# Summing four products of a weight pair in one PSUM bank, with ScalarE copies between, in a two-level feed-forward and mixer kernel

## The chip, the cores and the metric

The kernel runs on one core of a Trainium2 chip. The metric is the device time of one launch in microseconds (us), the median of several runs. Five engines work beside each other: TensorE (PE in the profile) multiplies into PSUM banks, VectorE (DVE), ScalarE (ACT) and GpSimd (POOL) work on tiles, and SyncE (SP) issues most of the DMAs.

## The reference, cut to what matters

One layer of a diffusion backbone over 1024 latent tokens and 256 context tokens, width 1024, in fp32. The three projections that the change touches are the inputs of the two feed-forward nets (1024 to 2 x 2816, then `silu(a) * b`) and the convolution and gate part of the mixers' input (1024 to 5 x 1024).

```python
def swiglu(h, w_in, w_out):
    a, b = jnp.split(h @ w_in, 2, axis=-1)
    return (jax.nn.silu(a) * b) @ w_out

def conv_branch(bg, cg, vc, conv_w):
    return bg * short_conv(cg * vc, conv_w)

x = x + 0.5 * ml[2] * swiglu(modulate(rms_norm(x, norm1_g), ml[0], ml[1]), ffn1_w_in, ffn1_w_out)
bg_l, cg_l, vc_l, q_l, k_l, v_l, gt_l = jnp.split(hx @ w_in, SPLITS, axis=-1)
g_conv, g_attn = jnp.split(jax.nn.sigmoid(gate_logits), 2, axis=-1)
x = x + ml[5] * merged
x = x + 0.5 * ml[8] * swiglu(modulate(rms_norm(x, norm3_g), ml[6], ml[7]), ffn2_w_in, ffn2_w_out)
```

## The kernel before, in words

Every fp32 product is made of three fp32r passes (high x high, high x low, low x high), so that one 128 x 512 output of 512 inputs takes 4 x 3 = 12 matmuls; `product` (line 683) issues them into one PSUM bank of its own. Each weight is split into a high part (a cast on ScalarE, tile `wl`) and a low part (a subtraction on VectorE, the same tile's second half); `wl` has four buffers, `raw` (the weights as loaded) three.

The class `Winograd` (line 487) computes the three projections with the seven-product scheme of Strassen and Winograd on 2 x 2 blocks: two halves of the tokens (C0 and C1) times two halves of the inputs, for a pair of 128-column weight blocks. The moving operands 0 to 7 (tiles `r`) are made once per stage in `norm0` and `norm1`; the weight sums `s1`, `s2`, `s3` are made per pair on GpSimd in `lefts` (line 613). There are three users: `half1` (first feed-forward, 22 pairs), `mix` (20 pairs) and `fast` (second feed-forward, 22 pairs). The first 13, 9 and 9 pairs of these have products 1 and 2 made **ahead**, while the norm of C1 is still being made (`start_by_half`, `start`), and their sums `u` (product 1) and `c` (products 1 + 2) kept: the first two on the chip, the others in DRAM (`ucd`), from where `fetch` (line 750) brings them back a pair early. An ahead pair thus has five products left, another pair seven.

For each pair the loop runs `next_first`, `second`, `third` (lines 758 to 776). They put the products in the order 6, 7, 4, 5, 3 (1 and 2 first where not ahead), each in one of five `ps` banks, and combine them on VectorE: u += 6, v = u + 7, b = v - 4, then v += 5, u += 5, u += 3. The results for C0 are c and b, those for C1 u and v. `spill` (line 1164) takes silu of one and multiplies, and stores the product; in `mix`, `mixed` and `gate` do the corresponding thing. From pair 14 (`SIDE_FROM`) on, `half1` also has `side` work: each weight that goes by serves the context tokens too, in a `po` bank, and product 0's weight is called for in between.

A scheduler fixes the order of every engine's instructions at build time; it follows the program order with freedom where data allow. On the chip each engine then works through its list in that order, waiting at each instruction for what it needs. Small generators (`steps`, `mix_steps`, `last_steps`) put the work of later stages, such as the modulation sums `macc` and the final loads, between the pairs.

Of the kernel before, what the change touches and what calls it, by code (L numbers as in the profile page):

```python
# [12 lines left out]
AF = mybir.ActivationFunctionType  # L13
# [27 lines left out]
SIDE_FROM = 14  # L41
# [10 lines left out]
def tile_dit_layer(  # L52
# [434 lines left out]
    class Winograd:  # L487
# [6 lines left out]
        def __init__(self, xs, gain, mod, m, pairs, plain=False, ahead=3, side_from=None):  # L494

            self.xs, self.gain, self.mod, self.m, self.plain = xs, gain, mod, m, plain
            self.halves, self.cols_a = [], [a for a, _ in pairs]
            self.r = {i: [None] * 4 for i in range(8)}
            self.side_from = side_from
            self.n_ahead, self.side, self.started, self.n_left = ahead, None, [], 0
            self.n_squares, self.accs = {}, {}
            self.source, self.ready = self.lefts(pairs, side_from), []

# [43 lines left out]
        def norm1(self, turned=None):  # L552
# [60 lines left out]
        def lefts(self, pairs, side_from):  # L613

            def cols(src):
                t = wpool.tile([P, SLOT], F32, tag="raw", name=uniq("raw"), bufs=3)
                load(t[:].rearrange("p (k n) -> p k n", n=P), src.rearrange("(k p) n -> p k n", p=P))
                return t[:, :512], t[:, 512:]
# [24 lines left out]
            for j, (wa, wb) in enumerate(pairs):  # L643
                side = side_from is not None and j >= side_from
                a, b = cols(wa), cols(wb)
# [4 lines left out]
                if j >= n:  # L650
                    yield from map(parts, a)
                yield parts(s2)
                yield parts(s3)
                if side:
                    yield parts(b[0])
                yield parts(b[1])
                yield parts(s1)
                pool.tensor_sub(out=s2, in0=a[1], in1=s2)
                yield parts(s2)
                if side_from is not None and j == side_from - 1:  # L660
                    for wa, wb in pairs[:side_from]:
                        yield from map(parts, cols(wa) + cols(wb))

        def prefetch(self, n, lo_engines=(None, None)):
            while len(self.ready) < n:
# [7 lines left out]
            self.prefetch(4)  # L673
            return self.ready.pop(0)

        def terms(self, ps, w, i, k):
            r = self.r[i][k]
            wh, wl = (w[:, v, k * P : (k + 1) * P] for v in range(2))
            matmul(ps, wh, r[:, 0], start=k == 0, stop=False)
            matmul(ps, wh, r[:, 1], start=False, stop=False)  # L680
            matmul(ps, wl, r[:, 0], start=False, stop=k == 3)

        def product(self, i):
            w, ps = self.left(), ps_s()
            for k in range(4):
                self.terms(ps, w, i, k)
            if self.side:
                self.side(i, w)
            return ps

        def first(self):

            u, c = ttile("u"), ttile("c")
            act.copy(out=u, in_=self.product(1))
            dve.tensor_add(out=c, in0=u, in1=self.product(2))
            return u, c

        def start(self, norm):

# [55 lines left out]
                    load(t, self.started[0][:, i])  # L755
                self.started[0] = u, c

        def next_first(self):
            if not self.started:
                return self.first()  # L760
            self.fetch()
            uc = self.started.pop(0)
            self.fetch()
            return uc

        def second(self, u):

            v, b = ttile("v"), ttile("b")
            dve.tensor_add(out=u, in0=u, in1=self.product(6))
            dve.tensor_add(out=v, in0=u, in1=self.product(7))  # L770
            if self.side:
# [12 lines left out]
    class Rows:  # L784

# [354 lines left out]
    def side(j, bank=ps_o):  # L1140
# [20 lines left out]

        return do

    def spill(a, b, j, ch):
# [9 lines left out]
    def context_out(j, banks=None, first=True, last=True):  # L1174
# [18 lines left out]
        for half in range(2):  # L1193
            for token in range(2):
# [3 lines left out]
                acc = c_acc[token][:, half * 512 : (half + 1) * 512]  # L1198
                dve.tensor_add(out=acc, in0=acc, in1=ps)

    for j in range(NH):
        half1.side = side(j) if j >= SIDE_FROM else None
        u, c = half1.next_first()
        v, b = half1.second(u)
        spill(c, b, j, C0)
        spill(*half1.third(u, v), j, C1)
# [94 lines left out]
        sp.dma_start(out=xc.t[i][:].rearrange("p a b -> p (a b)"), in_=cxd[i])  # L1301
    normc2 = modulated_norm(xc, h_ctx[0], h_ctx[1], CC, gain2, mods, 3)

    def mixed():
        u, a0 = mix.next_first()
        v, b0 = mix.second(u)
        a1, b1 = mix.third(u, v)
        return (C0, a0, b0), (C1, a1, b1)
# [462 lines left out]
    ]  # L1771

    fast.start(fast.norm1())
    for j in range(NH):
        if j > 1:
            run(last_steps, 3)
        u, c = fast.next_first()
        v, b = fast.second(u)
        spill(c, b, j, C0)
        spill(*fast.third(u, v), j, C1)  # L1780
    run(last_steps)
    gate3 = half_gate("gate3", 8)
    hs = Rows(hd, NH // 2, "hid")
# [76 lines left out]
```

## Time and profile before

| what | value |
|---|---|
| median of three runs | 2682.8 us (2680.39 to 2686.76) |
| the profiled execution's own time, and its span | 2685.79 us, 2684.0 us |
| mean granted TensorE clock | 0.995 |
| busy: PE, DVE, ACT, POOL | 98%, 75%, 44%, 21% |
| pairs: `half1` ahead / with side work | about 122 to 300 us / 457 to 677 us |
| pairs: `mix` | about 951 to 1250 us |
| pairs: `fast` | about 2072 to 2450 us |

A row of groups gives an engine, an operation, its tiles, how often (x), the sum in us and the mean in ns of one, then the idle time of the engine just before and what ended it. A row of windows gives the busy time of PE, PE's weight load, DVE, ACT and POOL in a stretch, then the clock, the share of DMA and GB/s. A row of the chain gives a start, a length, and the engine and tile that the end of the program was waiting for then.

### The profile page before, as it was taken

The numbers are of one execution on the slowest core, as the hardware profiler recorded it, in microseconds if no ns is written. First come the engines' busy times: TensorE is split into PE (matmuls) and PEld (weight loads), VectorE is DVE, ScalarE is ACT, GpSimd is POOL, SyncE is SP. The second block draws the span as 40 slices with busy tenths as digits, with TensorE's granted clock in tenths as the row PEclk, the third lists the DMA queues.
The fourth block names the chain that finished last, engine by engine and source line by source line (L and its number), as shares of the span: only waits on it lengthen the run. The fifth ranks groups of instructions, "written<-read, shape, count | busy, mean of one in ns | idle before, by whom it ended". The sixth has DMA issues, their size and how long they took to land.

```text
span 2684.0 us, 36956 instructions
## 1 busy us (share of the span) xinstructions
PE 2639.7 (98%) x13373; PEld 2221.6 (83%) x13373; DVE 2006.2 (75%) x3356; ACT 1171.3 (44%) x2317; POOL 557.9 (21%) x449
## 2 busy tenths in 40 slices
PE   8999999999999999999999999999999999999998
PEld 5787899888778878888999888887888788888888
DVE  5788966888877899877387676675668876667885
ACT  6533454433444633333245566673236233334453
POOL 0134201211010044333032112141001442330200
PEclk9999999999999999999999999999999999999999
DMA  8565465345974345242312532113734543228741
GB/s 317 194 204 177 144 221 173 109 130 209 288 182 122 111 158 180 95 130 75 103 48 91 87 87 64 32 44 110 262 100 144 181 154 95 86 88 288 182 90 64
DMA packets 370000, 376.93 MB, mean 140 GB/s; under 512 B 19590, under 2 KB 258328, under 8 KB 369816
## 3 DMA queue, kind: packets, MB, share of 16 engines
q1 hardware_dynamic: 359000, 353.03, 40.8%
q0 software_dynamic: 10816, 21.53, 4.9%
q8 instruction: 105, 1.72, 0.3%
q14 instruction: 79, 0.65, 0.1%
HBM read 306.78 MB, written 67.67 MB: 140 GB/s over the span
## 4 chain that ended last, share of the span: by engine, by line
PE 84%; DVE 4%; DMA 2%; issue 2%; POOL 1%; ACT 1%; SPq 0%; DVEq 0%; POOLq 0%; ACTq 0%
PE ps L90 69%; PE pt L90 7%; PE po L90 7%; DVE wl L90 1%; DMA raw<-in_ffn_w_in_dram 1%; DMA ws<-in_ffn_w_out_dram 1%; DVE r L90 1%; DMA rawm<-in_w_mod_dram 1%; POOL s L90 0%; DVE macc L90 0%; POOL ol L90 0%; DVE u L90 0%; DVE uc L90 0%; DVE nt L90 0%; DVE v L90 0%
## 5 line engine op out<-in xcount | busy, mean ns | idle before, releaser
L90 PE MATMUL ps<-r,wl 128*128 128x512 f32 x5196 | 1204.7, 391 | 12.2 <-DVE wl L90 5.3
L90 PEld LDWEIGHTS ps<-r,wl 128*128 128x128 f32 x5196 | 971.6, 188 | 221.9 <-DVE wl L90 7.9
L90 ACT CAST wl<-s 128x512 fp32r<-128x512 f32 x254 | 156.7, 619 | 322.6 <-PE ps L90 219.3
L90 POOL TENSOR_TENSOR s<-raw 128x512 f32<-128x512 f32 x64 | 93.4, 1459 | 891.2 <-DMA raw<-in_ffn_w_in_dram 380.9
L90 ACT CAST wl<-raw 128x512 fp32r<-128x512 f32 x287 | 177.5, 619 | 219.6 <-PE ps L90 157.3
L90 DVE TENSOR_TENSOR wl<-raw,wl 128x512 fp32r<-128x512 f32 x287 | 201.9, 705 | 62.1 <-ACT wl L90 59.6
L90 DVE TENSOR_TENSOR wl<-s,wl 128x512 fp32r<-128x512 f32 x254 | 229.8, 905 | 21.3 <-ACT wl L90 19.7
L90 POOL TENSOR_TENSOR s<-raw,s 128x512 f32<-128x512 f32 x64 | 103.9, 1624 | 362.3 <-DVE wl L90 362.3
L90 DVE SCALAR_TENSOR_TENSOR macc<-rawm,silu_c,macc 128x512 f32<-128x512 f32 x178 | 149.8, 858 | 31.7 <-DMA rawm<-in_w_mod_dram 30.7
L90 PE MATMUL ps<-wh,r 128*128 128x256 f32 x768 | 141.6, 285 | 0.0
L90 DVE TENSOR_TENSOR u<-u,ps 128x512 f32<-128x512 f32 x174 | 118.0, 678 | 28.7 <-PE ps L90 28.5
L90 DVE TENSOR_TENSOR pts<-pt,pts 128x512 fp32r<-128x512 f32 x160 | 108.7, 685 | 35.7 <-ACT pts L90 33.5
L90 ACT CAST pts<-pt 128x512 fp32r<-128x512 f32 x160 | 93.3, 595 | 94.8 <-PE pt L90 90.9
L90 DVE TENSOR_REDUCE m<-ps 128x1 f32<-128x512 f32 (+1 forms) x192 | 109.9, 594 | 23.3 <-PE ps L90 22.3
L90 ACT CAST rh<-hid 128x512 fp32r<-128x512 f32 x132 | 80.9, 620 | 101.6 <-PE ps L90 89.3
L90 PE MATMUL ps<-rh,wl 128*128 128x512 f32 x360 | 122.3, 390 | 2.8 <-ACT rh L90 2.8
L90 PEld LDWEIGHTS ps<-wh,r 128*128 128x128 f32 x768 | 120.6, 192 | 0.0
L90 PE MATMUL po<-pts,vh 128*128 128x512 f32 x256 | 111.4, 440 | 0.2 <-ACT pts L90 0.2
L90 PE MATMUL ps<-wl,r 128*128 128x256 f32 x384 | 108.8, 283 | 0.0
L90 ACT CAST wh<-raw 128x512 fp32r<-128x512 f32 (+1 forms) x85 | 67.9, 801 | 88.8 <-PE ps L90 57.8
L90 DVE TENSOR_TENSOR rl<-hid,rh 128x512 fp32r<-128x512 f32 x132 | 89.8, 684 | 20.2 <-PE ps L90 9.8
L90 PE MATMUL ps<-kl,qs 128*128 128x512 f32 x384 | 104.3, 395 | 0.0
(314 smaller groups left out, 5118.6 us busy)
## 6 DMA issues: line engine op xcount, KB each, us to landing
raw<-in_ffn_w_in_dram SPq DMA_DIRECT2D x130, 512.0 KB
raw<-in_ffn_w_out_dram SPq DMA_DIRECT2D x72, 512.0 KB
rawm<-in_w_mod_dram SPq DMA_DIRECT2D x136, 256.0 KB
raw<-in_w_in_dram SPq DMA_DIRECT2D x61, 512.0 KB
hid<-hd SPq DMA_DIRECT2D x40, 512.0 KB
ws<-in_ffn_w_out_dram POOLq DMA_DIRECT2D x30, 512.0 KB, 6.6
ucd<-uc SPq DMA_DIRECT2D x25, 512.0 KB
hd<-c SPq DMA_DIRECT2D x40, 256.0 KB
```

The source lines that it names most:

```text
L90: inst = getattr(self.engine, name)(*args, **kw)
```

## The change

Product 4's moving operand changes its sign (operand 4 is now f minus t2), so that product 4 can be added by TensorE. A pair now has two banks, x and z:

- x is opened by product 1, or for an ahead pair by a ScalarE copy of the kept `u` into the bank. Product 6 is added onto it; ScalarE copies the sum out (`u6`). Product 7 is added on; ScalarE copies the sum out (`v`). Product 4 is added on, and x is now b, which the multiply (or the sigmoid, into a tile of its own) reads from PSUM.
- z takes product 5, then v += z on VectorE; product 3 is added onto z, then u6 += z on VectorE.

The order of products is 5, 7, (side 0), then the head of the next pair (its 6 where ahead, its 1 and 2 elsewhere), 4, 3, then the next pair's 6 where that has not come yet. `order` in `lefts` writes this order for the weights, `results` for the products. Between pair 13 and pair 14 of `half1` the pairs stay apart. The three loops take results from the generator `results` instead of calling `next_first`, `second` and `third`.

```diff
@@ class Winograd
-                dve.tensor_sub(out=t2, in0=t2, in1=f[:, 1])
+                dve.tensor_sub(out=t2, in0=f[:, 1], in1=t2)
                 self.keep(4, k, t2)
...
-    def second(self, u):
-        v, b = ttile("v"), ttile("b")
-        dve.tensor_add(out=u, in0=u, in1=self.product(6))
-        dve.tensor_add(out=v, in0=u, in1=self.product(7))
-        if self.side:
-            self.side(0, self.left())
-        dve.tensor_sub(out=b, in0=v, in1=self.product(4))
-        return v, b
-    def third(self, u, v):
-        p5 = self.product(5)
-        dve.tensor_add(out=v, in0=v, in1=p5)
-        dve.tensor_add(out=u, in0=u, in1=p5)
-        dve.tensor_add(out=u, in0=u, in1=self.product(3))
-        return u, v
+    def head(self, j):
+        if j >= self.n_pairs:
+            return None
+        if j < self.n_ahead:
+            self.fetch()
+            u, c = self.started.pop(0)
+            x = ps_s()
+            act.copy(out=x, in_=u)
+            self.fetch()
+            return x, self.with_sixth(x), c
+        u, c = ttile("u"), ttile("c")
+        x = self.product(1, j=j)
+        act.copy(out=u, in_=x)
+        dve.tensor_add(out=c, in0=u, in1=self.product(2, j=j))
+        return x, None, c
...
+    def with_sixth(self, x):
+        u = ttile("u6")
+        act.copy(out=u, in_=self.product(6, x))
+        return u
+    def results(self, apart=None):
+        opened = self.tail(self.head(0))
+        for j in range(self.n_pairs):
+            x, u, c = opened
+            z, v = self.product(5), ttile("v")
+            act.copy(out=v, in_=self.product(7, x))
+            dve.tensor_add(out=v, in0=v, in1=z)
+            side = self.sides(j)
+            if side:
+                side(0, self.left())
+            if j + 1 != apart:
+                opened = self.head(j + 1)
+            self.product(4, x, j)
+            yield c, x
+            self.product(3, z)
+            dve.tensor_add(out=u, in0=u, in1=z)
+            if j + 1 != apart:
+                opened = self.tail(opened)
+            yield u, v
+            if j + 1 == apart:
+                opened = self.tail(self.head(j + 1))
...
-    def gate(dst, j, ch, g):
-        act.activation(out=g, in_=g, func=AF.Sigmoid)
+    def gate(dst, j, ch, src):
+        g = ttile("gate")
+        act.activation(out=g, in_=src, func=AF.Sigmoid)
```

The first place is ScalarE's list in the middle of `fast`'s ahead pairs. Before, one pair has its five weight casts (`wl_20094`, `wl_20114`, `wl_20132`, `wl_20164`, `wl_20182` for products 6, 7, 4, 5, 3) and the two silu, and no copy:

```order
L90 CAST wl_20094<-s_3717_20089 128x512
L90 CAST wl_20114<-s_3718_20090 128x512
L90 CAST wl_20132<-raw_20086 128x512
L90 CAST wl_20164<-s_3716_20088 128x512
L90 ACTIVATE c_20159<-c_20159 128x512
L90 ACTIVATE u_19925<-u_19925 128x512
L90 CAST wl_20182<-s_3717_20089 128x512
```

Now it reads as follows (`u_3561_19701` from its bank is a `u6`, `ps_19810` from `u` is the copy that opens the next x, `v_19677` is the copy after a product 7, `wl_19678` is the weight of a product 3, `wl_19702` and `wl_19718` those of the next pair's 5 and 7, `wl_19746` that of the 6 after):

```order
L90 CAST wl_19678<-s_3535_19534 128x512
L90 COPY v_19677<-ps_19590 128x512
L90 CAST wl_19702<-s_3550_19635 128x512
L90 COPY u_3561_19701<-ps_19695 128x512
L90 CAST wl_19718<-s_3552_19637 128x512
L90 COPY ps_19810<-u_19697 128x512
L90 ACTIVATE c_19698<-c_19698 128x512
L90 CAST wl_19746<-s_3567_19741 128x512
```

Three copies have come into each ahead pair's list, each behind at most one cast; the copy that opens a bank and the silu of the reloaded `c` stand ahead of the cast for that pair's product 6.

The second place is PE's list where `fast` begins. Before, products 6, 7, 4, 5 of the first pair run through each other in four banks (`ps_19706` is 6, `ps_19724` is 7, `ps_19751` is 4, `ps_19771` is 5), as the last quarter of each operand comes in:

```order
L90 MATMUL ps_19724<-r_3580_19416,wl_19665 128x512 x3
L90 MATMUL ps_19724<-r_3597_19483,wl_19665 128x512 x3
L90 MATMUL ps_19771<-r_3564_19352,wl_19703 128x512 x2
L90 MATMUL ps_19751<-r_3566_19359,wl_19682 128x512
L90 MATMUL ps_19751<-r_3583_19426,wl_19682 128x512 x3
L90 MATMUL ps_19751<-r_3600_19493,wl_19682 128x512 x3
L90 MATMUL ps_19724<-r_3612_19544,wl_19665 128x512
L90 MATMUL ps_19771<-r_3564_19352,wl_19703 128x512
L90 MATMUL ps_19771<-r_3581_19419,wl_19703 128x512 x3
```

Now (`ps_19526` is x, with `wl_19469` for 6 and `wl_19507` for 7; `ps_19559` is z, with `wl_19490` for 5):

```order
L90 MATMUL ps_19559<-r_3467_19243,wl_19490 128x512 x3
L90 MATMUL ps_19559<-r_3484_19310,wl_19490 128x512 x3
L90 MATMUL ps_19559<-r_3499_19371,wl_19490 128x512
L90 MATMUL ps_19526<-r_3500_19374,wl_19469 128x512
L90 MATMUL ps_19559<-r_3499_19371,wl_19490 128x512 x2
L90 MATMUL ps_19526<-r_3500_19374,wl_19469 128x512 x2
L90 MATMUL ps_19526<-r_3449_19173,wl_19507 128x512 x3
L90 MATMUL ps_19526<-r_3466_19240,wl_19507 128x512 x3
```

Only two products run through each other; 7 follows on the bank of 6 with nothing between them.

The third place is PE's list at the end of `fast`, products 7 (`wl_22174`) and 4 (`wl_22191`) of the last pair, which has no next pair behind it:

```order
L90 MATMUL ps_22124<-r_3483_19307,wl_22174 128x512 x3
L90 MATMUL ps_22124<-r_3498_19368,wl_22174 128x512 x3
L90 MATMUL ps_22124<-r_3452_19183,wl_22191 128x512 x3
L90 MATMUL ps_22124<-r_3469_19250,wl_22191 128x512 x3
L90 MATMUL ps_22124<-r_3486_19317,wl_22191 128x512 x3
```

Before, each product there had a bank of its own; now the copy of `v` has to come between the second and the third of these rows.

More of the change, by code (lines that the diff above doesn't have):

```diff
@@ L504, in __init__ @@
             self.side_from = side_from
-            self.n_ahead, self.side, self.started, self.n_left = ahead, None, [], 0
+            self.n_ahead, self.sides, self.started, self.n_left = ahead, lambda j: None, [], 0
+            self.n_pairs = len(pairs)
             self.n_squares, self.accs = {}, {}
@@ L642, in lefts, with fetch @@
                 yield from map(parts, cols(a))
-            for j, (wa, wb) in enumerate(pairs):
-                side = side_from is not None and j >= side_from
-                a, b = cols(wa), cols(wb)
+            state = {}
+            def fetch(j):
+                if j >= len(pairs) or j in state:
+                    return
+                a, b = map(cols, pairs[j])
                 s1, s2, s3 = ttile("s1"), ttile("s2"), ttile("s3")
@@ L1162, in side, with side_at @@
         return do
+    side_of = {}
+    def side_at(j):
+        if j is None or j < SIDE_FROM:
+            return None
+        if j not in side_of:
+            side_of[j] = side(j)
+        return side_of[j]
+    half1.sides = side_at
     def spill(a, b, j, ch):
@@ L1199, in context_out @@
                 dve.tensor_add(out=acc, in0=acc, in1=ps)
+    results = half1.results(SIDE_FROM)
     for j in range(NH):
[L1202 to L1206, printed above, removed]
+        for ch in (C0, C1):
+            spill(*next(results), j, ch)
         run(steps, STEPS[min(j, len(STEPS) - 1)])
@@ L1773, in tile_dit_layer @@
     fast.start(fast.norm1())
+    results = fast.results()
     for j in range(NH):
@@ L1776, in tile_dit_layer @@
             run(last_steps, 3)
[L1777 to L1780, printed above, removed]
+        for ch in (C0, C1):
+            spill(*next(results), j, ch)
     run(last_steps)
```

87 lines of the change are left out of this document (51 added, 36 removed).

## The prediction

> **What bounds the kernel now.** I read the page's busy times and its chain of waits first: which engine is the program waiting for?
>
> ```profile
> PE 2639.7 (98%) x13373; PEld 2221.6 (83%) x13373; DVE 2006.2 (75%) x3356; ACT 1171.3 (44%) x2317; POOL 557.9 (21%) x449
> PE 84%; DVE 4%; DMA 2%; issue 2%; POOL 1%; ACT 1%; SPq 0%; DVEq 0%; POOLq 0%; ACTq 0%
> 2295.00 182.27 PE ps L90 x804
> ```
>
> TensorE is busy for 98% of the span and owns 84% of the chain. The third row is an uninterrupted piece of the chain in the second feed-forward: 182.27 / 804 = 0.2267 us for one 128x512 matmul. So a product (12 matmuls) costs 2.72 us, an ahead pair (five products) 13.6 us, another pair (seven) 19.0 us. The change issues exactly the same matmuls: it can move the time only by the time in which TensorE waits. What waits does it have, and where? The waits of PE, then the windows of the stages that the change touches:
>
> ```profile
> PE ps L90 <- DVE wl L90: 5.3, 5, 2.8
> PE ps L90 <- ACT r L90: 3.5, 4, 1.6
> PE ps L90 <- ACT wl L90: 2.5, 4, 1.0
> ...
> 122.00:300.00 178.00, 172.93 (x751) 139.20 (x750) 143.53 (x203) 55.79 (x98) 68.80 (x46) 0.99 0.57 179
> 457.00:677.00 220.00, 220.00 (x1152) 187.24 (x1151) 175.08 (x269) 83.65 (x143) 39.45 (x27) 1.00 0.46 154
> 951.00:964.00 13.00, 9.54 (x38) 6.61 (x37) 12.84 (x18) 5.41 (x10) 5.52 (x3) 1.00 0.44 143
> 964.00:1250.00 286.00, 285.57 (x1261) 235.49 (x1261) 241.18 (x354) 92.79 (x163) 105.49 (x70) 1.00 0.41 130
> 2072.00:2093.00 21.00, 18.06 (x75) 13.59 (x75) 20.11 (x25) 8.69 (x16) 7.75 (x5) 1.00 0.33 112
> 2093.00:2447.00 354.00, 354.00 (x1563) 292.60 (x1563) 244.89 (x338) 116.34 (x193) 115.76 (x80) 1.00 0.42 131
> 2447.00:2475.00 28.00, 28.00 (x125) 23.21 (x124) 21.18 (x30) 12.46 (x22) 0.90 (x1) 1.00 0.98 361
> ```
>
> The windows are, in order: the first feed-forward's ahead pairs, its pairs with side work, the start of the mixers' projections, the rest of these, the start of the second feed-forward, the rest of it, and its end. In the three long ones TensorE stands still for 0, 0.43 and 0 us: nothing can be gained there. There are three places with idle time. Ahead pairs: 178.00 - 751 x 0.2267 = **7.75 us** (5.07 by the busy time alone). Start of the mixers: 13.00 - 9.54 = **3.46 us**, with VectorE busy 12.84 of 13.00. Start of the second feed-forward: 21.00 - 18.06 = **2.94 us**, VectorE 20.11 of 21.00. The whole sum is 14.2 us, 0.5% of the span, and that is the most that any relief of VectorE in these places can bring.
>
> **What the change removes and adds.** The groups of the combining instructions and of ScalarE's copies out of a bank:
>
> ```profile
> L90 DVE TENSOR_TENSOR u<-u,ps 128x512 f32<-128x512 f32 x174 | 118.0, 678 | 28.7 <-PE ps L90 28.5
> L90 DVE TENSOR_TENSOR v<-u,ps 128x512 f32<-128x512 f32 x58 | 39.5, 680 | 23.6 <-PE ps L90 23.5
> L90 DVE TENSOR_TENSOR b<-v,ps 128x512 f32<-128x512 f32 x64 | 43.8, 685 | 45.7 <-PE ps L90 44.4
> L90 ACT COPY u<-ps 128x512 f32<-128x512 f32 x33 | 19.4, 587 | 43.0 <-PE ps L90 36.3 <-DMA hd<-u 5.3 <-DVE u L90 1.3
> L90 ACT CAST wl<-s 128x512 fp32r<-128x512 f32 x254 | 156.7, 619 | 322.6 <-PE ps L90 219.3
> ```
>
> Each of the 64 pairs had six additions on VectorE after its products 6, 7, 4, 5 (two) and 3; now it has two. That is 64 x 4 x 0.68 = 174 us less for VectorE (2006 to 1832). ScalarE gets three copies in each of the 31 ahead pairs (u into x, u6, v) and two in the 33 others (u6, v; they copied product 1 before too): 159 x 0.59 = 94 us more (1171 to 1265). No row of before has ScalarE writing a bank; the nearest are its copy out of one, 0.587, and its cast between SBUF tiles, 0.619, and I take 0.59. None of it is on the path by itself, since both engines have room. What counts is the new order on bank x: 7 must wait for the copy after 6, and 4 for the copy after 7. Three cases:
>
> *Steady pairs: 0.* Between 6 and 7 TensorE has the previous pair's 4 and 3 and this pair's 5 (8.2 us); between 7 and 4 it has the next pair's 6 (2.72 us) or its 1 and 2 (5.4 us); between 5 and 3 at least three products. The copy of v stands behind at most one cast in ScalarE's list, so it ends about 0.62 + 0.59 = 1.21 us after product 7, and 2.72 covers it with 1.5 us to spare, the time of two more casts. Queued behind this copy are the casts for products three and four places on (8 us), so 0.59 does not reach TensorE. Without the cover, the price is 0.59 to 1.21 us a pair. The pairs with side work have 220.00 of 220.00 now and can only lose: between nothing and 0.59 in each of 8 pairs, 4.7 us; the cover is longer there, so I take 0.
>
> *Three places without cover.* The end of the second feed-forward: 4 follows 7 directly, because there is no next pair. ScalarE's list has three casts of the next weights ahead of that copy, which may be done by then: 0.59 at the least, 3 x 0.62 + 0.59 = 2.4 at the most, **+0.9** taken, nearest to the copy alone. The starts of the mixers and of the second feed-forward need the chain's rows:
>
> ```profile
> 954.03 0.63 ACT r L90
> 954.68 2.64 DVE r L90 x3
> ...
> 2077.09 5.21 DVE r L90 x5
> 2082.33 1.66 DVE nt L90
> 2084.01 0.63 ACT r L90
> 2084.66 0.69 DVE r L90
> ```
>
> Here TensorE waits for VectorE to make the last operands. Before, four products of the first pair were begun side by side, and three quarters of each, 36 matmuls, were there to do meanwhile. Now there are only 6 and 5 (18 matmuls): 7 comes after 6 is whole and copied. At 2085.4 us, when the last operand is ready, before has nearly all 48 matmuls behind it; after would have 24 and part of 7. If the operands for 6 and 5, which stand first in VectorE's order, let 7 begin near 2083, TensorE is one product (2.72 us) behind, and gets back the 0.9 us that the rest of this window loses now (7.00 - 6.14 between 2086 and 2093): **+1.8**. Bounds: -2.94 (all idle time goes, as VectorE has fewer additions) to 24 x 0.2267 = +5.4.
>
> ```profile
> 2086.00:2093.00 7.00, 6.14 (x27) 4.78 (x26) 6.83 (x10) 2.59 (x5) 1.30 (x1) 1.00 0.10 37
> ```
>
> At the mixers' start the operands come within 5 us (954 to 958.9), so less work can be put off: **+0.4**, one exposed copy less a part of VectorE's relief; bounds -3.46 to +2.72, one product.
>
> The Trainium skill, "PSUM — Partial Sum Buffer", section "PSUM bank collisions raise a hardware error", says that no two engines may touch a bank in the same partitions at once, so that the copy can't run beside the next product's matmuls into the same bank. By that rule the three exposed copies cost their full length; if a copy could overlap the next product's first matmuls, the sum would be lower by up to 3 x 0.59 = 1.8 us. No run here shows such an overlap.
>
> *Ahead pairs of the first feed-forward.* This is where a gain can come from. VectorE is busy 143.53 of 178.00 us and loses 13 x 4 x 0.68 = 35 us of work. But what does TensorE wait for there? Four successive pieces of the chain of this window:
>
> ```profile
> 256.38 5.42 DMA raw<-in_ffn_w_in_dram
> 261.83 1.27 POOL s L90
> 263.19 2.86 POOL s L90 x2
> 266.07 0.63 ACT wl L90
> ```
>
> It is a weight load, then GpSimd's sums, then a cast; VectorE enters only because it holds the raw buffers until the low part is made, and through `macc`. So its relief lets loads start sooner, but does not shorten them. I take half of the 7.75: **-3.9**. Bounds: -7.75, and on the other side each of the 11 reloaded pairs' casts later by one copy, 11 x 0.59 = +6.5.
>
> **Sum.** -3.9 (ahead pairs) + 0.4 (mixers' start) + 1.8 (second feed-forward's start) + 0.9 (its end) = -0.8 us. From the profiled execution's 2685.8 that is 2685.0. That execution lay 3.0 us above the median of the runs (2682.8), so the forecast is **2682 us**. The likeliest case's own range is 2674 to 2691, not all bounds being reached at once.
>
> **Rivals.**
>
> *VectorE's relief counts fully (faster).* All of the 7.75 goes, and the mixers' start and the second feed-forward's lose half their idle time instead of gaining waits (-1.7 and -1.5), the end +0.9: -10, **2673 us**. For it: VectorE is over 95% busy in both starts. Against: in the largest place the chain shows loads and GpSimd. Chance 0.22.
>
> *The copy that opens x blocks ScalarE (slower).* That copy needs the reloaded `u`, and stands ahead of the casts for that pair's 6 and 4. Before, only silu of the reloaded `c` could block so:
>
> ```profile
> ACT c L90 <- DMA c<-ucd: 53.6, 13, 8.5
> ```
>
> Thirteen waits of 4.1 us on average, and TensorE is hardly touched by them, as weights are split two to three products in advance. Now `u` must be there before 6 instead of after it. The case decides where the reload lands so late that the cast for 6 is not done when TensorE comes: that is from 2.72 us (one product of cover) on. With 13 such waits, 13 x (4.1 - 2.72) = +18 us, **2700 us**; with half of them 2691. For it: the first feed-forward moves 179 GB/s and its loads take over 5 us. Against: `c`'s waits occur in the same places now, without loss. Chance 0.20.
>
> *The starts lose a whole product or two.* Upper bounds at both starts, +2.7 and +5.4, with the gain of -3.9 gone: +9.0, **2692 us**. Chance 0.13.
>
> *The change does nothing.* The waits of the ahead pairs are the loads' alone and stay as they are, the starts come out even, the end +0.9: **2684 us**. Chance 0.12.
>
> *The clock falls.* The row of the ahead pairs shows 0.99, the others 1.00, even across the wait of 2.8 us. If new short waits at the bank changes let the granted clock go to half for the time of one pair, it costs 13.6 us: **2696 us**. Chance 0.03. The Trainium skill, "TensorE: Matmul & The Clock Gate", section "A second HAM failure mode: psum-queue depth-cycling", describes that: small idle times between groups of matmuls that cycle through PSUM banks make the clock swing between half and full. The trace speaks against it so far, with 1.00 over 354 us of such cycling.
>
> **How the numbers follow.** The forecast's case has 0.30. The lower end of the range takes in the fast rival with a margin of 2 us: 2671. The upper end is between the slow rival's half and whole price: 2698. Outside lie about 0.06 below and 0.11 above. About 0.2%, 5.4 us, is what a measurement of this kernel can tell from no change: below 2677.4 lie most of the fast rival and a little of the forecast's case, 0.24; above 2688.2 the two slow rivals, the clock and a little of the forecast's, 0.33; between them 0.43.
>
> **What would show it.** VectorE near 1832 and ScalarE near 1265 us busy. PE full (at most 0.5 us idle) in the windows of the steady pairs; a wait of PE for ScalarE's `v` in these would refute the cover. PE waits named `u` or `v` at the two starts and once at the end, under 1.3 us each. In the ahead pairs of the first feed-forward idle time about half of now, with loads and GpSimd still in the chain; if it vanishes, VectorE was the cause. New waits of ScalarE at the bank for the reload of `u`, followed by PE waiting for `wl`, would be the slow rival.

## The result and the profile after

The changed kernel takes 2722.6 us (median of four runs, 2719.1 to 2723.5), the kernel before 2682.8: a ratio of 1.0145, 95% interval 1.0127 to 1.0162. It is **40 us slower**; the forecast was no change, and its range ended at 2698. The profiled execution took 2722.1 us with a span of 2720.3, 36.3 us more than that of before. The page's busy times:

```profile
PE 2652.5 (98%) x13373; PEld 2228.0 (82%) x13373; DVE 1847.0 (68%) x3100; ACT 1250.0 (46%) x2476; POOL 541.4 (20%) x449
```

VectorE and ScalarE do as much as was worked out (1832 and 1265 foreseen), and the matmuls are the same 13373. But they keep TensorE busy 12.8 us longer (2652.5 against 2639.7), and it stands still 23.5 us longer (2720.3 - 2652.5 = 67.8, before 2684.0 - 2639.7 = 44.3). So there are two losses: new waits, and slower matmuls. Where are they? The windows of the changed kernel, cut at the same matmuls as the six windows of before in the prediction (first feed-forward ahead, with side work; mixers' start, rest; second feed-forward's start, rest):

```profile
123.20:306.80 183.60, 174.52 (x751) 141.87 (x750) 105.07 (x149) 74.33 (x134) 65.55 (x48) 0.97 0.53 173
465.10:694.20 229.10, 222.07 (x1152) 187.44 (x1150) 153.93 (x237) 91.51 (x158) 36.91 (x27) 0.99 0.45 151
968.10:984.80 16.70, 10.74 (x38) 7.71 (x36) 9.38 (x15) 5.57 (x11) 9.09 (x4) 0.90 0.35 126
984.80:1280.10 295.30, 290.00 (x1261) 237.54 (x1262) 198.89 (x281) 111.00 (x204) 96.88 (x69) 0.99 0.39 125
2099.60:2123.70 24.10, 21.09 (x75) 15.71 (x74) 16.47 (x20) 9.35 (x17) 11.96 (x8) 0.86 0.38 120
2123.70:2485.10 361.40, 355.71 (x1564) 292.24 (x1563) 201.66 (x257) 139.98 (x242) 110.24 (x78) 1.00 0.41 132
```

| stage | before | after | difference | forecast |
|---|---|---|---|---|
| first feed-forward, ahead pairs | 178.0 | 183.6 | +5.6 | -3.9 |
| first feed-forward, side work | 220.0 | 229.1 | +9.1 | 0 |
| mixers, start | 13.0 | 16.7 | +3.7 | +0.4 |
| mixers, rest | 286.0 | 295.3 | +9.3 | 0 |
| second feed-forward, start | 21.0 | 24.1 | +3.1 | +1.8 |
| second feed-forward, rest and last products | 354.0 | 361.4 | +7.4 | +0.9 |

The six make 38.2 of 36.3 us; what lies between them gives 2 back. In each stage VectorE is less busy than before (105 us for 144 in the first row), and in all but one TensorE waits more: at the start of the second feed-forward it stands still for 3.01 us as against 2.94, and the 3.1 us there are slower matmuls (21.09 us busy for the same 75, before 18.06; granted clock 0.86). What does it wait for? The waits of PE in the changed kernel:

```profile
PE ps L90 <- DVE wl L90: 12.6, 7, 3.4
PE ps L90 <- ACT v L90: 8.5, 5, 3.2
PE pt L90 <- ACT acch L90: 6.3, 1, 6.3
```

Few waits make most of it: seven for VectorE's half of the weights (5.3 us before), five for the copy of v, one for a modulation sum behind the last pair of the first feed-forward. One of them in time, from the timeline of the changed kernel (start, length, engine; in brackets the idle time before and what ended it):

```profile
225.12 0.75 DVE L90 SCALAR_TENSOR_TENSOR macc<-rawm,silu_c,macc 128x512 f32<-128x512 f32 x1 [2.50 <-DMA rawm<-in_w_mod_dram]
225.79 0.68 DVE L90 TENSOR_TENSOR wl<-s,wl 128x512 fp32r<-128x512 f32 x1
225.91 0.59 ACT L90 COPY v<-ps 128x512 f32<-128x512 f32 x1 [3.81 <-DVE macc L90]
...
226.53 1.75 PE L90 MATMUL ps<-r,wl 128*128 128x512 f32 x6 [3.39 <-DVE wl L90]
```

VectorE has come to `macc` before the load `rawm` has landed, and stands 2.50 us. Behind it in its list is the low half of the next weight. ScalarE waits as well: its copy of `v` reads product 7, which is done when TensorE stops at 223.1 us, and writes a buffer of the ring of eleven temporaries. The trace names that `macc` as what ended its wait, so it waited for the buffer and not for the product. Then TensorE starts again, but how fast? Three windows around the next such wait, of 2.73 us, ended by `wl` at 272.4 us:

```profile
269.50:272.40 2.90, 0.22 (x1) 0.00 (x0) 1.35 (x2) 0.00 (x0) 0.00 (x0) 0.99 0.93 287
272.40:275.60 3.20, 3.15 (x7) 2.48 (x8) 2.04 (x3) 1.11 (x2) 0.00 (x0) 0.50 0.83 314
275.60:278.80 3.20, 3.20 (x15) 2.66 (x14) 2.63 (x2) 1.49 (x3) 1.65 (x2) 0.98 0.51 166
```

After the wait the granted clock is 0.50 for some 3.2 us: 7 matmuls go where 15 go after it. Such a wait costs itself and some 1.6 us more. The trace of the changed kernel has 12 stretches at half clock, 51 us in all, that of before 5, 21 us. TensorE is busy in most of the 30 us more and does half the work in them, which is about the 12.8 us of longer busy time.

### The profile page after: what moved, and what is told of

Read it like the earlier page. It is cut to its first block, busy times and chain, and to the rows that moved or that the text cites. A ratio compares the mean times of both kernels' runs of the same rounds, so it can differ in the third digit from the quotient of the medians.

```text
span 2720.3 us, 36840 instructions
## 1 busy us (share of the span) xinstructions
PE 2652.5 (98%) x13373; PEld 2228.0 (82%) x13373; DVE 1847.0 (68%) x3100; ACT 1250.0 (46%) x2476; POOL 541.4 (20%) x449
## 4 chain that ended last, share of the span: by engine, by line
PE 53%; DMA 3%; DVE 2%; issue 2%; POOL 1%; ACT 1%; DVEq 0%; SPq 0%; ACTq 0%; POOLq 0%
PE ps L90 44%; PE pt L90 5%; PE po L90 4%; DMA rawm<-in_w_mod_dram 1%; DVE wl L90 0%; DMA c<-ucd 0%; DMA hd<-u 0%; DVE u L90 0%; DVE r L90 0%; DMA raw<-in_ffn_w_out_dram 0%; POOL ol L90 0%; POOL s L90 0%; DVE y L90 0%; DMA hd<-c 0%; DVE macc L90 0%
## 5 line engine op out<-in xcount | busy, mean ns | idle before, releaser
L90 PE MATMUL ps<-r,wl 128*128 128x512 f32 x5196 | 1218.9, 394 | 29.8 <-DVE wl L90 12.2
L90 DVE TENSOR_TENSOR wl<-s,wl 128x512 fp32r<-128x512 f32 x254 | 201.9, 796 | 136.6 <-ACT wl L90 135.5
L90 DVE TENSOR_TENSOR wl<-raw,wl 128x512 fp32r<-128x512 f32 x287 | 229.8, 803 | 65.7 <-ACT wl L90 64.5
L90 POOL TENSOR_TENSOR s<-raw 128x512 f32<-128x512 f32 x64 | 86.9, 1358 | 903.1 <-DVE wl L90 247.0
L90 DVE SCALAR_TENSOR_TENSOR macc<-rawm,silu_c,macc 128x512 f32<-128x512 f32 x178 | 132.2, 765 | 68.6 <-DMA rawm<-in_w_mod_dram 67.1
L90 POOL TENSOR_TENSOR s<-raw,s 128x512 f32<-128x512 f32 x64 | 92.5, 1446 | 412.5 <-DVE wl L90 411.9
L90 ACT COPY v<-ps 128x512 f32<-128x512 f32 x64 | 37.5, 587 | 164.7 <-PE ps L90 111.7
L90 DVE TENSOR_TENSOR v<-v,ps 128x512 f32<-128x512 f32 x64 | 43.8, 684 | 89.6 <-ACT v L90 88.7
```

The costliest lines, as they stand in the source:

```text
L90: inst = getattr(self.engine, name)(*args, **kw)
```

## The experiments

Each run was compared with runs of the kernel before on the same chip, and its difference is taken to those. Two theories stood against each other at first. A: each stage pays for slack of its own that it has lost. B: the temporaries are held longer and push the modulation work back through the program.

**One stage at a time (e1 to e3).** The class gets a switch, and two of the three users keep the separate banks, the additions and the order of before (shown for e1):

```diff
-    mix = Winograd(xs, None, modl, 3, column_pairs(wi, mix_offsets), plain=True, ahead=AH2)
+    mix = Winograd(xs, None, modl, 3, column_pairs(wi, mix_offsets), plain=True, ahead=AH2, merged=False)
...
-    fast = Winograd(xs, None, modl, 6, column_pairs(ffn2_w_in[0], ffn_offsets), ahead=AH3)
+    fast = Winograd(xs, None, modl, 6, column_pairs(ffn2_w_in[0], ffn_offsets), ahead=AH3, merged=False)
```

> Only the first feed-forward sums in one bank; the mixers and the second feed-forward keep the separate banks and the VectorE additions. Theory A (each stage pays for its own lost slack: product 4 waits for the copy of v with 2.72 us of cover, and that copy waits for buffers and loads): the 8.8 us of the ahead pairs and the 9.4 us after the last pair stay, later stages as before: about 2700 us. Theory B (the temporary buffers held longer push the modulation sums back through the whole program): part of the loss of later stages stays too, above 2706 us.

> Only the mixers' projections sum in one bank. Theory A: the 12 to 13 us that the trace shows between 950 and 1110 us, and nothing elsewhere: about 2695 us. Theory B: less than half of it, under 2690 us, since the sums that were late in the first feed-forward come in time.

> Only the second feed-forward sums in one bank. Theory A: its own 10 us (start 4.3, three waits for v or its weights 4.0, end 2.0): about 2692 us. Theory B: only the start and the end, about 2688 us or less.

Measured 2702.8, 2702.5 and 2696.4 us beside 2686.8 of before: +16.0, +15.8 and +9.6 (ratios 1.0060, 1.0058, 1.0041 with intervals of about 0.0015 to each side). The sum is 41.4 for the 40 of the whole (each interval is some 4 us to each side). The profile of e1, cut at the same matmuls, has all its loss in the first feed-forward (8.4 us in the ahead pairs, 8.9 in those with side work). So the stages pay separately, as A says, and nothing is seen to be carried on. But A's reason does not hold for the first feed-forward: there TensorE waits for weights and for `acch`, and hardly for v. Three rows of PE's waits in e1:

```profile
PE ps L90 <- DVE wl L90: 12.6, 7, 3.3
PE pt L90 <- ACT acch L90: 6.4, 1, 6.4
PE ps L90 <- ACT v L90: 1.5, 2, 0.9
```

**One temporary less in each pair (e4, e5).** The copy after product 6 (e4) or the copy after 7 (e5) goes into the tile of `u` (the edits are shortened to what matters, here and below):

```diff
-            u = ttile("u6")
-            act.copy(out=u, in_=self.product(6, x))
+            act.copy(out=u, in_=self.product(6, x))    # e4, with the old u
...
-                z, v = self.product(5), ttile("v")
+                z, v = self.product(5), opened_u    # e5
```

> The whole change, but the copy after product 6 goes into the tile of u instead of a new temporary: one buffer of the ring of eleven less in each pair. Theory A: the waits are those of v's copy behind late loads, and stay: 2715 to 2725 us. Theory B: at least half of the 40 us is given back: 2705 us or less.

> The whole change, but the copy of v after product 7 goes into the tile of u, which nobody reads any more then, instead of a new temporary; so it can't wait for the last reader of an older temporary. Theory C (that copy waits for its buffer, which a late modulation sum on VectorE still holds, and TensorE waits for the copy): PE's waits for v (8.5 us), with what the clock loses after them, go: 2705 to 2712 us. Theory D (ScalarE's or VectorE's list itself is blocked by something late, whatever buffer v has): 2718 us or more.

Measured 2727.0 beside 2686.8 (+40.2) and 2736.9 beside 2686.3 (+50.6). B fell with e4. In e5 theory C was that v's copy waits for its ring buffer and that this wait is the loss; it fell too. The waits of PE in e5:

```profile
PE ps L90 <- ACT wl L90: 15.1, 9, 4.4
PE ps L90 <- DVE wl L90: 13.9, 14, 4.3
PE pt L90 <- ACT acch L90: 9.8, 1, 9.8
PE ps L90 <- ACT u L90: 6.5, 7, 1.9
```

Both copies now write a tile called u, so the last row holds the waits for either. Together they fell from 10.0 us (8.5 for `v`, 1.5 for `u`) to 6.5, but the waits for weights rose from 15.5 us (12.6 and 2.9) to 29.0. So v's buffer alone is not the cause; the reading that both lists are late, and that v is one of the places where it shows, fits but is not shown by this.

**More cover (e6), and product 4 apart (e18).** In e6 an ahead pair's 5 comes ahead of the 4 of the pair before it; in e18 the order is that of the change, but 4 has its own bank:

```diff
                 if j + 1 != apart:
                     opened = self.head(j + 1)
+                    early = self.product(5)                                     # e6
-                self.product(4, x, j)
+                dve.tensor_add(out=b, in0=v, in1=self.product(4, j=j))          # e18
```

> The whole change, but an ahead pair's product 5 is also put before product 4 of the pair ahead of it: 5.4 us of other work between 7 and 4 instead of 2.72. If the short cover is what lets ScalarE's lateness through, the losses in the ahead pairs of all three stages (about 9, 8 and 4 us) fall by half or more: about 2712 us. If the weights (VectorE's wl) are late and not v, nothing is gained: 2720 us or more.

> The whole change with its order and overlap, but product 4 goes into a bank of its own and VectorE makes b = v + 4, so that nothing follows 7 on bank x. If the chain 7, copy of v, 4 is where lateness reaches TensorE, PE's waits for v (8.5 us) and the slow clock behind them go: 2703 to 2711 us. If lateness reaches it through weights and the rest of the lists anyway, 2716 us or more.

Measured 2748.3 beside 2686.3 (+62) and 2755.1 beside 2685.7 (+69.4, ratio 1.0254, 1.0234 to 1.0274). Had the short cover been the cause, both would have helped; instead they are among the three slowest of all. Each expectation had this as its other outcome, for late weights; but in e6 it is not the weights that TensorE waits for. There, twice the cover gives four times the wait for v, by its row among PE's waits:

```profile
PE ps L90 <- ACT v L90: 36.3, 12, 6.3
```

Two of these copies, from ScalarE's timeline in e6:

```profile
213.72 0.58 ACT L90 COPY v<-ps 128x512 f32<-128x512 f32 x1 [6.50 <-DMA hd<-u]
2181.86 0.58 ACT L90 COPY v<-ps 128x512 f32<-128x512 f32 x1 [5.29 <-DVE macc L90]
```

These copies do not wait for product 7 at all. They wait for the buffer of the ring, which a store to DRAM (`hd` from `u`) or a late modulation sum still reads. In e18, with one temporary (b), one bank and VectorE's addition for it more, TensorE waits for ScalarE's copy `u` (in the ahead pairs that is `u6`) and its casts; PE's longest waits in e18:

```profile
PE ps L90 <- ACT u L90: 15.1, 12, 3.3
PE ps L90 <- ACT wl L90: 13.6, 11, 3.2
```

So the step from 7 over the copy to 4 isn't the cause by itself. Running more of the next pair earlier costs more. What made e18 slower, of the three things that it adds, is not shown.

**Without the modulation loads (e7, e8, e15).** In the later modulation sums seven of eight loads and multiply-adds are left out, in the changed kernel, in the kernel before, and in the version without overlap below:

```diff
             for k in range(KD):
+                if k:
+                    yield
+                    continue
                 raw = ttile("rawm")
```

> The whole change, with part of the work left out: of the eight loads and multiply-adds of each later modulation sum only the first is done, so the layer is computed with other modulations. To be read against the next run, the kernel before with the same left out. If late modulation loads, which VectorE waits for in order, are the cause, the two differ by 15 us at most (the starts, the end and the mixers' weights); if the change loses by its own chain of products, they differ by 30 us or more.

> The kernel before with the same modulation loads and multiply-adds left out, as the base of the run ahead of it. TensorE waits little for them in the kernel before: 2670 to 2683 us.

> Sums in one bank without overlap of pairs (as in e11), and without the modulation loads and multiply-adds that e7 and e8 leave out, so other modulations are used. To be read against e8 (2667 us). If the overlap and the loads are the whole loss, 2667 to 2674 us. If the chain of copies in one bank costs by itself, 2680 us or more.

Measured 2695.0 against 2667.0: 28 us between the changed kernel and the kernel before, where it is 40 with the loads. It lies between the two expectations (15 at most, 30 or more), and e8 is 3 us under its own: about 12 us hang on the modulation loads, 28 do not. VectorE's own waits for these loads had grown with the change; the row of before and the row of the changed kernel:

```profile
DVE macc L90 <- DMA rawm<-in_w_mod_dram: 42.5, 29, 3.8
```

```profile
DVE macc L90 <- DMA rawm<-in_w_mod_dram: 73.5, 46, 4.3
```

e15 took 2682.2, which is 15 us over e8, so the second of its two expectations came: even without overlap and without these loads the sums in one bank cost something. (The kernel before took 2685.1 us beside e15 and 2686.3 beside e8.)

**Modulation work elsewhere (e9, e14, and the same in the kernel before: e13, e17).** In e9 and e13 the modulation work of the first feed-forward stands between a pair's C0 and C1 result, in e14 and e17 each pair with side work gets 16 steps of it for 11:

```diff
-            spill(*next(results), j, ch)
-        run(steps, STEPS[min(j, len(STEPS) - 1)])
+        spill(*next(results), j, C0)
+        run(steps, STEPS[min(j, len(STEPS) - 1)])    # e9, e13
+        spill(*next(results), j, C1)
...
-STEPS = (0, 6, 6, 6, 6, 6, 6, 6, 6, 6, 6, 6, 6, 0, 11)
+STEPS = (0, 6, 6, 6, 6, 6, 6, 6, 6, 6, 6, 6, 6, 0, 16)    # e14, e17
```

> The whole change, but in the first feed-forward the modulation work of a pair is put between its C0 and its C1 result, so that it stands where it stood before the change with respect to products, and not behind the next pair's product 6 or 1 and 2. If the 6.3 us wait after the last pair (product pt from acch) comes from modulation work that has slid back in the program, it goes: 2710 to 2716 us. If the chain of products is the cause, nothing changes: 2720 us or more.

> The kernel before, with only the modulation work of the first feed-forward put between a pair's C0 and C1 result (the edit that cost the changed kernel another 24 us). If any move of that work costs some 20 us, whatever the products' banks (the order just fitted before), the kernel before loses 15 us or more: above 2700 us. If the separate banks let TensorE ride over late lists, it loses under 8 us: 2683 to 2692 us.

> The whole change, with 16 instead of 11 modulation steps behind each pair with side work, so that this work is done before the last pair. If the wait for acch behind the last pair (6.3 us and the slow clock after it, 9 us together) comes from its late end, it goes: 2712 to 2716 us. If not, 2720 us or more.

> The kernel before with 16 instead of 11 modulation steps behind each pair with side work, the edit of e14. If the separate banks let TensorE ride over late lists, the kernel before loses under 5 us: 2678 to 2690 us. If this much modulation work is too much for these pairs whatever the banks are, 2695 us or more.

| edit | changed kernel, to before | kernel before, to itself |
|---|---|---|
| none | +40 | 0 |
| work between C0 and C1 | e9: 2748.2, +63.6 | e13: 2677.7, **-7.4** (ratio 0.9975, 0.9965 to 0.9984) |
| 16 steps | e14: 2738.6, +53.5 | e17: 2684.1, -1.6 (ratio 0.9990, 0.9980 to 1.0000) |

The same two edits cost the changed kernel 24 and 13 us more, and the kernel before nothing. (e13 was expected to lose up to 8 us; that it gains was not foreseen.) So it is not that any move of this work costs; it is the changed kernel that has no room for it. The windows of the ahead pairs in e9 and then in e13, at the same matmuls:

```profile
121.70:323.10 201.40, 179.84 (x752) 144.03 (x751) 119.85 (x163) 74.84 (x137) 66.45 (x47) 0.92 0.50 160
```

```profile
123.20:292.10 168.90, 168.90 (x751) 138.71 (x750) 139.42 (x202) 56.11 (x98) 68.51 (x46) 1.00 0.60 188
```

e13 has all of VectorE's additions, VectorE busy for 139.42 of 168.90 us, and TensorE does not stand still once. e9 has fewer and loses 32 us to it in the same work. For the pairs with side work, e14 and then e17:

```profile
467.90:710.30 242.40, 228.76 (x1152) 192.66 (x1151) 154.72 (x245) 93.35 (x160) 35.72 (x26) 0.96 0.42 135
```

```profile
459.70:681.30 221.60, 220.55 (x1150) 187.52 (x1149) 174.80 (x277) 84.33 (x144) 42.93 (x26) 1.00 0.47 156
```

The single wait for `acch` did go in e9 and in e14, as was expected, and the time rose all the same: in e14 waits for v came for it, more of them than in the changed kernel (8.5 us, 5 times) and longer; their row in e14:

```profile
PE ps L90 <- ACT v L90: 21.7, 9, 6.0
```

**Starts and end apart (e10), VectorE copies v (e12).**

```diff
+                if j in self.apart_at:    # e10: first pair of mix and fast, last of fast
+                    dve.tensor_add(out=v, in0=u, in1=self.product(7))
+                    ...
+                    dve.tensor_add(out=b, in0=v, in1=self.product(4))
...
-                act.copy(out=v, in_=self.product(7, x))
+                dve.tensor_copy(out=v, in_=self.product(7, x))    # e12
```

> The whole change, but in the first pair of the mixers and of the second feed-forward, and in the last pair of the latter, products 7 and 4 go into banks of their own again. If the places without cover are what costs there, the losses at the starts (about 7 and 4 us) and at the end (2 us) go: 2708 to 2713 us. If these starts lose for late weights or operands, under 4 us is given back: 2718 us or more.

> The whole change, but v is copied out of its bank by VectorE, not ScalarE: ScalarE's list is as long as before but for two copies. If ScalarE's list is what makes 4 wait, PE's waits go down by half: 2705 to 2712 us. If VectorE's list is blocked in the same places (modulation loads), 2718 us or more, with PE waiting for VectorE's v instead.

Measured 2721.1 and 2740.7 beside 2684.6: +36.5 and +56. The places without cover, on which the prediction spent most of its words, are worth some 3 us of the 40 at most, and with intervals of about 5 us these 3 can't be told from nothing. And ScalarE is no worse than VectorE as the copier: moved there, the waits go along (TensorE waits 10.7 us for VectorE's `v`).

**No overlap of pairs (e11, e16).** Each pair runs 6, 5, 7, 3, 4, with 3 in a third bank, so that every copy keeps one product of cover:

```diff
+                z, v = self.product(5), ttile("v")
+                act.copy(out=v, in_=self.product(7, x))
+                dve.tensor_add(out=v, in0=v, in1=z)
+                dve.tensor_add(out=u, in0=u, in1=z)
+                opened = self.open()
+                dve.tensor_add(out=u, in0=u, in1=self.product(3))
+                self.product(4, x, j)
```

> Sums in one bank, but no overlap of pairs: each pair runs 6, 5, 7, 3, 4, with 3 in a third bank, so that every copy still has 2.72 us of cover, the operands of the next pair are not needed earlier, and buffers are held no longer than before. VectorE has one addition more in a pair than with the change. If the overlap is what costs (weights and buffers needed earlier, other work behind), 2690 to 2700 us. If the cover of one product is too short by itself, 2715 us or more.

> Sums in one bank without overlap (e11) with 16 modulation steps a pair (e14). Both theories of the loss together: if they add, 2697 to 2704 us, still not under the kernel before. If the losses move with every reordering instead, 2706 us or more.

Measured 2706.5 beside 2684.6 (+21.9, ratio 1.0074, 1.0057 to 1.0092), between the two expectations, and 2709.7 beside 2685.1 (+24.6). Without overlap 18 of the 40 us go. The windows of the mixers' rest and of the second feed-forward's rest in e11:

```profile
978.20:1267.90 289.70, 286.79 (x1262) 234.90 (x1261) 211.13 (x297) 110.03 (x203) 107.38 (x71) 1.00 0.40 130
2114.30:2470.90 356.60, 355.27 (x1563) 292.37 (x1562) 204.51 (x271) 136.88 (x238) 111.72 (x79) 1.00 0.41 133
```

They lose 3.7 and 2.6 us to before where the change loses 9.3 and 7.4. The other 22 us remain; with e7, e8 and e15 beside it, some 15 us are left that need neither the overlap nor the loads, and what they are no run shows.

e16 looks as if the 16 steps were nearly free without overlap (+24.6 for +21.9). The windows of the pairs with side work, where the edit lies, say otherwise; e11 and then e16:

```profile
466.00:690.20 224.20, 221.68 (x1152) 187.10 (x1150) 158.74 (x243) 88.30 (x157) 40.35 (x26) 1.00 0.43 145
461.60:695.57 233.97, 225.32 (x1152) 188.82 (x1151) 161.91 (x251) 89.86 (x158) 39.47 (x26) 0.99 0.43 144
```

The 16 steps cost these pairs 9.8 us with the sums in one bank and no overlap, and 13.3 with overlap (242.4 in e14, 229.1 in the changed kernel), but 1.6 with a bank for each product (221.6 in e17, 220.0 before). e16's total hides it, since its ahead pairs ran 6 us shorter than those of e11. So for this edit it is the shared bank, more than the overlap, that takes the room away (one profile of each kernel).

## Why the prediction was wrong, point by point

- *TensorE is the bound, and only its waits can move.* Right, but only half of it was counted. The sum took matmuls at 0.2267 us throughout; 12.8 of the 36.3 us are matmuls at half clock behind the waits. The clock stood among the rivals, with 0.03, as swings from many short waits. What came are half-clock stretches of some 3.4 us, most of them behind single waits of 2.3 us or more. The price could have been read from the kernel before, inside the very window of 0.99: behind a wait of 1.35 us for `sq_acc` at 292 us there is one such stretch, which the mean over 178 us hides:

```profile
295.00:298.40 3.40, 3.40 (x10) 2.63 (x9) 3.40 (x5) 1.17 (x3) 1.67 (x1) 0.50 0.27 97
```

The Trainium skill, "TensorE: Matmul & The Clock Gate", section "What's actually happening", gives half clock after an idle window of about 3.4 us; the traces here differ in the length: waits of 2.3 to 3.2 us mostly had it behind them too (the window with 0.50 at 272.4 us follows one of 2.73 us), and the measured waits are what counts for this kernel.
- *VectorE's and ScalarE's busy times.* Right within 15 us each. The copy into a bank, of which before had no row, takes 0.592 us for the 0.59 taken; its row among the groups of the changed kernel:

```profile
L90 ACT COPY ps<-u 128x512 f32<-128x512 f32 x25 | 14.8, 592 | 54.3 <-DMA u<-ucd 54.1
```
- *"Steady pairs: 0."* This is **the step that failed**. It compared the cover of 2.72 us with a chain of 1.21 us whose links were all busy times of ScalarE. But the copies also wait for the buffer that they write, held by a late modulation sum or a store: 3.81 us at 225.91 in the changed kernel, 6.50 in e6, and in a steady pair of the mixers 7.25 us, where TensorE stands 3.19 us behind it. The copy and the matmul behind it in the changed kernel:

```profile
1107.66 0.59 ACT L90 COPY v<-ps 128x512 f32<-128x512 f32 x1 [7.25 <-DVE macc L90]
1108.30 2.29 PE L90 MATMUL ps<-r,wl 128*128 128x512 f32 x5 [3.19 <-ACT v L90]
```

The prediction had named what is queued behind the copy, not what the copy's own target waits for; and it had named such a wait of PE for `v` as what would refute its cover. Measured: +9.1 in the side pairs, 6.3 of it the wait for `acch` behind the last of them; +9.3 in the mixers; +5.7 in the second feed-forward (7.4 less the 1.71 at its end), in all 24 us for the 0 foreseen. Waits for v are only some 6 of the 24; the wait for `acch`, of which the prediction had no term, is as much, and half clock is most of the rest.
- *Ahead pairs of the first feed-forward, -3.9.* Wrong in sign: +5.6. The idle time there was not VectorE's load. e13 removes all of it and leaves VectorE as it is; the change relieves VectorE and makes it longer. What came are three waits for VectorE's half of the weights, 8.4 us together, two of them behind a `macc` whose load was late (2.50 and 2.39 us).
- *Starts and end, +3.1 together.* Starts +3.7 and +3.1; e10 gives back only 3 us of all with the products apart. The exposed copies of `u6` were there as foreseen, 0.73 us each, but they are not what the starts lost. At the mixers' start, +3.7 lies beyond the bound of +2.72: TensorE waits 2.94 us for a weight cast, which in its turn waits for GpSimd's sum, as ScalarE's timeline shows:

```profile
984.18 0.62 ACT L90 CAST wl<-s 128x512 fp32r<-128x512 f32 x1 [5.36 <-POOL s L90]
```

At the second feed-forward's start the idle time is as before and the 3.1 us are matmuls at half clock, so that +1.8 came near them is luck. At the end the copy of v came behind three casts, as was worked out, the last of which had waited 2.09 us for its load, and TensorE waited 1.71 us for the 0.9 foreseen, by its timeline in the changed kernel:

```profile
2479.49 0.73 PE L90 MATMUL ps<-r,wl 128*128 128x512 f32 x2 [1.71 <-ACT v L90]
```

The sizes were right to a few us and mattered little; of the reasons, only the one at the end and the 0.73 us of each exposed copy held.
- *The rivals.* The slow one had the mechanism nearest to what came (a copy of ScalarE that is late for something that the profile of before shows only without harm, and TensorE behind it), but tied to the reload of `u`. Those waits came as described (54.1 us in the row above, for the 53.6 of `c` before), but TensorE waited only once, for 2.9 us, for a cast of ScalarE's, and that is the cast above, which waited for GpSimd; the waits that hurt were for `v`, for `acch` and for VectorE's half of the weights.

**What is shown:** the loss adds up over the stages; 12 us need the modulation loads; 18 go without the overlap; slower matmuls make a third of it (12.8 of 36.3); the same edits to the modulation work that cost the changed kernel 24 and 13 us cost the kernel before nothing, and the second of them, the 16 steps, costs 9.8 us in the pairs that it concerns with one bank and no overlap. So the changed kernel stands late lists worse than the kernel before. **What is argued:** why it does. Before, each product had a bank of its own, and a late addition on VectorE was met only when five banks were full; now two or three copies a pair stand in ScalarE's list between the weight casts, two of them tied to a ring buffer, and a late one holds back weights and products alike. **What stays open:** which of these ties costs how much, and what the 15 us are that need neither overlap nor loads. Taking away single ties (e4, e5, e10, e12, e18) moved the waits and lowered the time in one case only, by 3 us, which is within the noise. A longer ring of temporaries or a fourth buffer for raw weights would be the direct test; it was not tried.

The experiments point to a version that beats both kernels: e13, the kernel before with the modulation work between the two results, 2677.7 us.

## What to carry to other kernels

Where one engine is busy for 98% of the span, fewer instructions on another engine are worth at most the waits that it causes, and a new order is to be judged by what it does to lateness: how far can each list slip until the busy engine stands still? For an instruction that is new on the path, look up what its output buffer waits for, not only its input and its queue. And try the order of side work before taking work away: that alone removed the idle time that the relief was meant to remove.

## What the runs showed of the hardware

A wait of TensorE can cost more than itself. In the changed kernel the granted clock went to 0.50 with nine of the ten waits of 2.3 to 6.3 us (the one ahead of the first matmul aside), mostly for 3.4 us, in which 7 or 8 matmuls took 0.43 us each for 0.23: some 1.6 us on top. That price is not fixed. In the kernel before only one of four waits of 2.3 to 3.6 us had it, but waits of 1.32, 1.35 and 1.95 us did. Counted over the traces of all twenty kernels here, half clock followed 37 of 132 waits of 1 to 2 us, 67 of 92 of 2 to 3 us and 56 of 58 longer ones. Shorter waits close behind each other can do it too: after four of 0.37 to 0.95 us between 2103.9 and 2109.4 us in the changed kernel the clock was 0.50 for 6.8 us.
